# Splitting the left factors of the products of halves two at a time, from blocks side by side in one raw tile

## The chip, the cores and the metric

The kernel runs on one core of a Trainium2 chip. The time is device time in microseconds (us) of one execution; the kernel before took 1882.66 us, the median of 3 runs (1881.72 to 1883.4). One further execution was taken with the hardware profiler.

## What is computed

A decoder trunk of two layers on 512 tokens and 16 meta tokens in front of them, width 1024, everything in float32. Layer 0 mixes the tokens with gated linear attention, layer 1 with sliding-window attention on keys and values made after layer 0. Each layer has a feed-forward block (width 2816) before and after the mixer. Cut to what matters here:

```
def swiglu(x, w_in, w_out):
    gate, up = jnp.split(x @ w_in, 2, axis=-1)
    return (jax.nn.silu(gate) * up) @ w_out

for layer in range(DEPTH):
    h = h + 0.5 * rmsnorm(swiglu(rmsnorm(h, g[0]), w_ffn_in[layer, 0], w_ffn_out[layer, 0]), g[1])
    hn = rmsnorm(h, g[2])
    ...
    h = h + rmsnorm(mix, g[3])
    h = h + 0.5 * rmsnorm(swiglu(rmsnorm(h, g[4]), w_ffn_in[layer, 1], w_ffn_out[layer, 1]), g[5])
```

## The kernel before

**Operands in two parts.** TensorE multiplies in a reduced float32 format, so every operand is kept as a high part (the rounded value) and a low part (what is left), and each product is three matmuls: high by high, low by high, high by low. A weight comes from memory into a raw buffer by a DMA on SP's queue. ScalarE writes its high part (a copy with a rounding), and VectorE then writes its low part (raw less high). The text calls the two instructions a split. The pool `rp` has 8 raw buffers of 128 x 512, the pool `hp` 32 buffers of two times 528 columns ("slots", tag `pair`), which also hold the activations.

**The feed-forward block.** `ffn` works through the 22 hidden tiles of 128 in four chunks of 4, 6, 6 and 6 (`FF_CHUNKS`). After each chunk its part of the down projection follows (`out_steps`). The first chunk is computed plainly. The three others are the stretches that the change touches: there each hidden tile has a gate and an up weight (128 x 1024 each), and the two projections of the two halves of the tokens are computed with seven products of halves instead of eight (Strassen's scheme in the form with few additions). The left factors of the seven are sums of four blocks of the weights: r11 and r12 are the two halves of the gate weight, r21 and r22 those of the up weight. They have the names 11, 12, 22 and s1 = r21+r22, s3 = r11+r21, s2 = s3+r22, s4 = r12+s2. A product is 12 matmuls (4 blocks of 128 rows, three matmuls each), 264 columns wide in layer 0 and 256 in layer 1. The text calls a gate weight with its up weight a pair; a chunk has six pairs.

**The chain of a pair.** `split_pair` (L249) makes the seven factors: split 11, add r21 to r11 and r22 to r21 in place (L264), split s1, split s3, add r22 to r11, split s2, split 12, add r11 to r12, split s4, split 22. The high parts are L258, the low parts L259. In the profile the products' left factors that were added up are named `w_s`, the others `w`. For the other weights the split is L239 and L240.

**The products.** `Strassen.product` (L881) waits until a factor has been written out by the planner, issues the 12 matmuls and gives one slot back (`free_slots`). The order on TensorE is 11, s1, s2, 12, s3, then 11 of the next pair, then s4 and 22, so `head` (11), `body` and `tail` of two pairs interlock. Their results are gathered by L904 (a to d), L910, L912 and L914 on ScalarE and by L917, L926, L932 and L933 on VectorE; L927 is the SiLU, L936 and L937 write the hidden tile's two parts. L912 must have read bank a before s3 is added to it, L917 before 22 is.

**What sets the order.** TensorE's instructions run in the order of the program text. `Flow` is a planner at build time: its clock advances with every matmul, and jobs (generators) emit their instructions when their time has come; `yield STEP` puts 1.1 us of that clock between two steps of a chain. The other engines' instructions are put in order by the compiler, by readiness, starting from the order in which they were emitted; each engine then runs its list strictly in order. `load_unit` (L287) takes the next weight's raw buffers, issues its DMAs and starts its chain; `prefetch` calls it while the slots asked for stay within `ahead` (16) of those given back, with at most two chains of pairs at once (`CHAINS`). `slot` (L227) lets a chain take a slot only while fewer than the limit (`RING`, 10 in these stretches) are out. A raw buffer is given to the next load when its last reader is done.

Of the kernel before, what the change touches and what calls it, by code (L numbers as in the profile page):

```python
# [9 lines left out]
F32 = mybir.dt.float32  # L10
F32R = mybir.dt.float32r
I32 = mybir.dt.int32
AF = mybir.ActivationFunctionType
ALU = mybir.AluOpType
AX = mybir.AxisListType

P = 128
# [12 lines left out]
L1 = [(16, 256), (272, 256)]  # L30
L1W = [(16, 512)]
SLOTS = 32
RAWS = 8
RING = 10
STEP = 1.1
CHAINS = 2
# [101 lines left out]
def trunk_kernel(ctx: ExitStack, tc, a, out, last_out):  # L138
    nc = tc.nc
    pe, act, dve, pool, sp = nc.tensor, nc.scalar, nc.vector, nc.gpsimd, nc.sync  # L140
    flow = Flow()

    cp = ctx.enter_context(tc.tile_pool(name="cp", bufs=1))
    rp = ctx.enter_context(tc.tile_pool(name="rp", bufs=RAWS))
    hp = ctx.enter_context(tc.tile_pool(name="hp", bufs=SLOTS))
# [14 lines left out]
    def pair_tile(name, dt=F32R):  # L160
        return hp.tile([P, 2, TOK], dt, tag="pair", name=name)
# [5 lines left out]
    def flat(t):  # L167
        return t.rearrange("p a t -> p (a t)")
# [58 lines left out]
    def slot(i):  # L227

        while live[0] + sum(n for j, n in owed.items() if j < i) >= limit[0]:
            yield room[0]  # L230
        live[0] += 1
        owed[i] -= 1

    def raw_tile(name):
        return rp.tile([P, 512], F32, tag="raw", name=name)

    def split_part(i, raw, m):
        w = pair_tile(f"w{i}_{len(loaded[i])}")
# [7 lines left out]
            yield from slot(i)  # L246
            split_part(i, raw, m)

    def split_pair(i, raws):  # L249


        r11, r12, r21, r22 = raws
        parts, ready = loaded[i]

        def part(name, src):
            yield from slot(i)
            w = pair_tile(f"w{i}_{name}")
            act.activation(w[:, 0, :512], src, AF.Copy)  # L258
            dve.tensor_tensor(w[:, 1, :512], src, w[:, 0, :512].bitcast(F32), op=ALU.subtract)  # L259
            parts[name].append(w)  # L260
            ready[name].finish(flow)

        def add(dst, src):
            dve.tensor_tensor(dst, dst, src, op=ALU.add)  # L264

        yield 2.2
        yield from part("11", r11)
        add(r11, r21)
        add(r21, r22)
        yield STEP  # L270
        yield from part("s1", r21)
        yield STEP
        yield from part("s3", r11)
        add(r11, r22)
        yield STEP
        yield from part("s2", r11)
        yield STEP
        yield from part("12", r12)
        add(r12, r11)
        yield STEP  # L280
        yield from part("s4", r12)
        yield STEP
        yield from part("22", r22)
        chains[0] -= 1
        prefetch()

    def load_unit():  # L287
        i = len(loaded)
        asked[0] += costs[i]
        owed[i] = costs[i]  # L290
        if isinstance(units[i], list):
            g, u = units[i]
            chains[0] += 1
            raws = [raw_tile(f"raw{i}_{k}") for k in range(4)]
            for k in (2, 0, 1, 3):
                sp.dma_start(raws[k], (g, u)[k // 2][:, k % 2 * 512 : (k % 2 + 1) * 512])
                dma_end[0] = max(dma_end[0], flow.clock) + 512 * 1.5e-3
            names = ("11", "12", "22", "s1", "s2", "s3", "s4")
            loaded.append(({k: [] for k in names}, {k: Job(None) for k in names}))
            gen = split_pair(i, raws)  # L300
        else:
            n = units[i].shape[-1]
            raws = []
            for c in range(0, n, 512):
                m = min(512, n - c)
                raws.append((raw_tile(f"raw{i}_{c}"), m))
                sp.dma_start(raws[-1][0][:, :m], units[i][:, c : c + m])
            dma_end[0] = max(dma_end[0], flow.clock) + n * 1.5e-3
            loaded.append([])
            gen = split_unit(i, raws)  # L310
        split_jobs.append(flow.spawn(gen, dma_end[0] - flow.clock))

    def prefetch():
        while len(loaded) < cap[0] and asked[0] + costs[len(loaded)] <= freed[0] + ahead[0]:
            if isinstance(units[len(loaded)], list) and chains[0] == CHAINS:
                break
            load_unit()
# [16 lines left out]
    def free_slots(n):  # L334
        freed[0] += n
        live[0] -= n
        room[0].finish(flow)
        room[0] = Job(None)
        prefetch()
# [531 lines left out]
    class Strassen:  # L871
# [9 lines left out]
        def product(self, bank, t, left, right, first):  # L881
            parts, ready = t.pair
            flow.wait(ready[left])
            w = parts[left][0]
            for k in range(4):
                wh, wl = (w[:, i, k * P : (k + 1) * P] for i in range(2))
                xh, xl = (self.z[right][k // 2][:, i, k % 2] for i in range(2))
                mm(bank, wh, xh, first and k == 0, False, not first)
                mm(bank, wl, xh, False, False, not first)
                mm(bank, wh, xl, False, k == 3, not first)  # L890
                flow.pump()
            free_slots(1)

        def head(self, hid):
            t = Job(None)
# [571 lines left out]
    raws = [[raw_tile(f"raw{i}_{c}") for c in (0, 512)] for i in range(2)]  # L1467
# [156 lines left out]
```

## Time and profile before

| | us |
|---|---|
| median of 3 runs | 1882.66 |
| profiled execution | 1881.52 |
| its span, first to last instruction | 1879.7 |
| ScalarE: high parts of the pairs' factors (L258) | 175.2 + 133.9 |
| VectorE: low parts of the pairs' factors (L259) | 193.8 + 148.3 |
| VectorE: adds of blocks (L264) | 198.0 |
| VectorE waiting for the high parts of added factors | 128.7 |

The sums of L258 and L259 are over 288 factors `w_s` and 216 factors `w`, 72 pairs of seven. In the lines of the profile PE is TensorE's matmuls, PEld its weight loads, DVE VectorE, ACT ScalarE, POOL GpSimd and SP the engine that issues the DMAs. A line of a group has line, engine, operation, what is written and read, shapes and count, then busy time and mean duration of one in nanoseconds, then the idle time in front of them and whom the engine waited for. A line of a timeline has the start in us from the beginning of the span, the time taken, and the instruction; in brackets stands the idle time in front of it. Neighbouring instructions of one kind are merged, with their count. A matmul's duration there overlaps with its neighbours', so the distance of starts is what counts.

### The profile page before, as it was taken

The page shows a single profiled execution, that of the slowest core. Times are in us where ns is not written, and L with a number is a line of the kernel's source. Part 1 is how long each engine was busy: PE and PEld are TensorE (multiplying, and loading weights), DVE is VectorE, ACT ScalarE, POOL GpSimd, SP SyncE. Part 2 cuts the span into 40 slices and gives each one's busy share as a digit, 9 for nine tenths or more (in the row PEclk, how much of TensorE's full clock was granted, in tenths as well). Part 3 has the DMA queues.
Part 4 walks back from the last instruction along what each step waited for, and adds up shares of the span by engine and source line. Part 5 has one row for each costly group of instructions (what it writes and reads, how often), then busy time and mean ns, then how long its engine had stood idle before and what let it go on. Part 6 is the DMA issues. An engine that isn't in the chain of part 4 may idle for free.

```text
span 1879.7 us, 37270 instructions
## 1 busy us (share of the span) xinstructions
PE 1866.2 (99%) x14479; PEld 1784.8 (95%) x14479; DVE 1396.2 (74%) x2829; ACT 1026.9 (55%) x2311; POOL 163.9 (9%) x297
## 2 busy tenths in 40 slices
PE   9999999999999999999999999999999999999998
PEld 8999999999999999999999898989987898989898
DVE  7885858767564788585887886868766779868585
ACT  6663535654446566363574553536757855636364
POOL 2000000330001300000033000000320140000002
PEclk9999999999999999999999999999999999999999
DMA  5333233421213123232351223333421212333331
GB/s 170 99 96 101 92 105 96 138 68 57 68 57 113 46 90 108 90 102 91 109 168 46 73 88 110 93 110 101 136 74 52 69 46 73 99 104 104 102 113 60
DMA packets 102273, 174.70 MB, mean 93 GB/s; under 512 B 11856, under 2 KB 24016, under 8 KB 102096
## 3 DMA queue, kind: packets, MB, share of 16 engines
q1 hardware_dynamic: 101664, 171.74, 29.3%
q8 instruction: 113, 1.85, 0.4%
q10 hardware_dynamic: 432, 0.59, 0.1%
q14 instruction: 64, 0.52, 0.1%
HBM read 169.66 MB, written 2.10 MB: 91 GB/s over the span
## 4 chain that ended last, share of the span: by engine, by line
PE 85%; DVE 8%; ACT 4%; issue 2%; DMA 0%; POOL 0%; DVEq 0%; SPq 0%; ACTq 0%; POOLq 0%
PE y L175 31%; PE x L175 20%; PE a L175 17%; PE c L175 7%; PE d L175 4%; DVE raw L264 2%; ACT w_s L258 2%; DVE w_s L259 2%; DVE w L259 2%; PE o L175 1%; PE e L175 1%; PE po L175 1%; DVE w L240 1%; DVE hidl1f L937 1%; ACT s L1350 0%
## 5 line engine op out<-in xcount | busy, mean ns | idle before, releaser
L259 DVE TENSOR_TENSOR w_s<-raw,w_s 128x512 fp32r<-128x512 f32 x288 | 193.8, 690 | 131.0 <-ACT w_s L258 128.7
L175 PE MATMUL y<-hidl0f,w 128*128 128x256 f32 (+1 forms) x2112 | 261.4, 285 | 0.3 <-DVE hidl0f L451 0.3
L175 PEld LDWEIGHTS y<-hidl0f,w 128*128 128x128 f32 x2112 | 259.0, 188 | 0.7 <-DVE hidl0f L451 0.5
L240 DVE TENSOR_TENSOR w<-raw,w 128x512 fp32r<-128x512 f32 x376 | 235.3, 654 | 31.3 <-ACT w L239 29.1
L258 ACT ACTIVATE w_s<-raw 128x512 fp32r<-128x512 f32 x288 | 175.2, 628 | 152.3 <-DVE raw L264 139.5
L175 PE MATMUL y<-hidl1f,w 128*128 128x512 f32 (+1 forms) x1344 | 251.2, 346 | 0.4 <-DVE hidl1f L937 0.3
L175 PEld LDWEIGHTS y<-hidl1f,w 128*128 128x128 f32 x1344 | 212.5, 188 | 35.1 <-DVE hidl1f L937 1.6
L239 ACT ACTIVATE w<-raw 128x512 fp32r<-128x512 f32 x376 | 207.0, 586 | 41.4 <-PE y L175 29.3
L264 DVE TENSOR_TENSOR raw<-raw,raw 128x512 f32<-128x512 f32 x288 | 198.0, 687 | 5.5
L445 POOL TENSOR_TENSOR acc_post<-acc_post,sq_post 128x256 f32<-128x256 f32 (+1 forms) x77 | 63.3, 822 | 1537.1 <-ACT sq_post L444 1536.4
L259 DVE TENSOR_TENSOR w<-raw,w 128x512 fp32r<-128x512 f32 x216 | 148.3, 687 | 30.0 <-ACT w L258 29.2
L258 ACT ACTIVATE w<-raw 128x512 fp32r<-128x512 f32 x216 | 133.9, 621 | 41.6 <-PE y L175 41.3
L175 PE MATMUL x<-x_l0m,w 128*128 128x272 f32 (+1 forms) x1152 | 152.0, 288 | 0.0
L175 PEld LDWEIGHTS x<-x_l0m,w 128*128 128x128 f32 x1152 | 143.2, 188 | 2.7 <-issue 1.7
L701 DVE TENSOR_TENSOR Y<-y,Y 128x256 f32<-128x256 f32 (+2 forms) x175 | 81.8, 474 | 71.2 <-PE y L175 70.8
L175 PE MATMUL a<-zl0f_t,w_s 128*128 128x264 f32 x864 | 117.3, 285 | 0.0
L175 PE MATMUL a<-zl1f_t,w_s 128*128 128x256 f32 x864 | 114.3, 281 | 1.1 <-ACT c L912 0.7
L175 PEld LDWEIGHTS a<-zl0f_t,w_s 128*128 128x128 f32 x864 | 110.1, 188 | 0.3
L175 PEld LDWEIGHTS a<-zl1f_t,w_s 128*128 128x128 f32 x864 | 107.2, 188 | 2.9 <-ACT c L912 2.6
L175 PE MATMUL x<-x_l0f,w 128*128 128x256 f32 (+1 forms) x768 | 98.1, 287 | 1.2 <-ACT w L239 0.7
L175 PEld LDWEIGHTS x<-x_l0f,w 128*128 128x128 f32 x768 | 94.8, 188 | 2.5 <-DVE w L240 1.1
L175 PE MATMUL x<-x_l1f,w 128*128 128x256 f32 (+1 forms) x576 | 93.1, 320 | 0.0
(516 smaller groups left out, 3219.9 us busy)
## 6 DMA issues: line engine op xcount, KB each, us to landing
raw<-in_w_in SPq DMA_DIRECT2D x352, 256.0 KB, 2.9
raw<-in_w_out SPq DMA_DIRECT2D x96, 256.0 KB, 3.3
raw<-in_w_last SPq DMA_DIRECT2D x48, 256.0 KB, 3.0
raw<-in_gla_in SPq DMA_DIRECT2D x48, 256.0 KB, 3.3
raw<-in_w_out SPq DMA_DIRECT2D x64, 128.0 KB, 2.9
raw<-in_gla_out SPq DMA_DIRECT2D x16, 256.0 KB, 2.7
raw<-in_w_q SPq DMA_DIRECT2D x16, 256.0 KB, 4.2
raw<-in_swa_out SPq DMA_DIRECT2D x16, 256.0 KB, 3.4
```

Of the source, the lines that this page charges most:

```text
L175: inst = pe.matmul(o, lhs, rhs, start=start, stop=stop, skip_group_check=onto)
L239: act.activation(w[:, 0, :m], raw[:, :m], AF.Copy)
L240: dve.tensor_tensor(w[:, 1, :m], raw[:, :m], w[:, 0, :m].bitcast(F32), op=ALU.subtract)
L258: act.activation(w[:, 0, :512], src, AF.Copy)
L259: dve.tensor_tensor(w[:, 1, :512], src, w[:, 0, :512].bitcast(F32), op=ALU.subtract)
L264: dve.tensor_tensor(dst, dst, src, op=ALU.add)
L445: pool.tensor_tensor(sums[0][:, :n], sums[0][:, :n], t[:, :n], op=ALU.add)
L701: dve.tensor_tensor(y, p[:, :n], y, op=ALU.add)
L937: dve.scalar_tensor_tensor(t.hid[:, 1, g], t.h, -1.0, t.hid[:, 0, g].bitcast(F32), op0=ALU.mult, op1=ALU.subtract)
```

## The change

The raw pool has two tiles of 2048 columns in place of eight of 512. `raw_tile` hands out quarters of the current tile; a pair takes a whole one. A pair's four blocks lie in it in the order r21, r11, r12, r22, in which they are also loaded. `split_pair` splits 11 alone, as before, and then two factors at a time, from two blocks that lie side by side: s1 with s3, s2 with 12, s4 with 22. Each is one ScalarE instruction and one VectorE instruction of 1024 columns. The high parts of two factors go into one slot and their low parts into another. The adds stay as they were. `product` takes the high and low part from two places, and gives slots back when both factors that share them are used: one after 11, two after 12, s3 and 22. In the planner's time the steps of the chain lie where the first factor of each two lay.

```diff
--- before.py
+++ after.py
@@ -30,7 +30,7 @@
 L1 = [(16, 256), (272, 256)]
 L1W = [(16, 512)]
 SLOTS = 32
-RAWS = 8
+RAWS = 2
 RING = 10
 STEP = 1.1
 CHAINS = 2
@@ -231,8 +231,15 @@
         live[0] += 1
         owed[i] -= 1
 
-    def raw_tile(name):
-        return rp.tile([P, 512], F32, tag="raw", name=name)
+    quarters = [None, 4]
+
+    def raw_tile(name, n=1):
+
+        if quarters[1] + n > 4:
+            quarters[:] = rp.tile([P, 2048], F32, tag="raw", name=name), 0
+        t, i = quarters
+        quarters[1] += n
+        return t[:, i * 512 : (i + n) * 512]
 
     def split_part(i, raw, m):
         w = pair_tile(f"w{i}_{len(loaded[i])}")
@@ -246,41 +253,42 @@
             yield from slot(i)
             split_part(i, raw, m)
 
-    def split_pair(i, raws):
-
-
-        r11, r12, r21, r22 = raws
+    def split_pair(i, raw):
+
+
+
         parts, ready = loaded[i]
-
-        def part(name, src):
-            yield from slot(i)
-            w = pair_tile(f"w{i}_{name}")
-            act.activation(w[:, 0, :512], src, AF.Copy)
-            dve.tensor_tensor(w[:, 1, :512], src, w[:, 0, :512].bitcast(F32), op=ALU.subtract)
-            parts[name].append(w)
-            ready[name].finish(flow)
+        r21, r11, r12, r22 = (raw[:, k * 512 : (k + 1) * 512] for k in range(4))
+
+        def two(names, k):
+            hi, lo = [], []
+            n = len(names)
+            for _ in names:
+                yield from slot(i)
+            ws = [flat(pair_tile(f"w{i}_{name}")) for name in names]
+            hi, lo = (ws[0][:, :1024], ws[1][:, :1024]) if n == 2 else (ws[0][:, :512], ws[0][:, 512:1024])
+            src = raw[:, k * 512 : (k + n) * 512]
+            act.activation(hi, src, AF.Copy)
+            dve.tensor_tensor(lo, src, hi.bitcast(F32), op=ALU.subtract)
+            for c, name in enumerate(names):
+                parts[name] += [t[:, c * 512 : (c + 1) * 512] for t in (hi, lo)]
+                ready[name].finish(flow)
 
         def add(dst, src):
             dve.tensor_tensor(dst, dst, src, op=ALU.add)
 
         yield 2.2
-        yield from part("11", r11)
+        yield from two(["11"], 1)
         add(r11, r21)
         add(r21, r22)
         yield STEP
-        yield from part("s1", r21)
-        yield STEP
-        yield from part("s3", r11)
+        yield from two(["s1", "s3"], 0)
         add(r11, r22)
-        yield STEP
-        yield from part("s2", r11)
-        yield STEP
-        yield from part("12", r12)
+        yield 2 * STEP
+        yield from two(["s2", "12"], 1)
         add(r12, r11)
-        yield STEP
-        yield from part("s4", r12)
-        yield STEP
-        yield from part("22", r22)
+        yield 2 * STEP
+        yield from two(["s4", "22"], 2)
         chains[0] -= 1
         prefetch()
 
@@ -291,13 +299,13 @@
         if isinstance(units[i], list):
             g, u = units[i]
             chains[0] += 1
-            raws = [raw_tile(f"raw{i}_{k}") for k in range(4)]
-            for k in (2, 0, 1, 3):
-                sp.dma_start(raws[k], (g, u)[k // 2][:, k % 2 * 512 : (k % 2 + 1) * 512])
+            raw = raw_tile(f"raw{i}", 4)
+            for c, k in enumerate((2, 0, 1, 3)):
+                sp.dma_start(raw[:, c * 512 : (c + 1) * 512], (g, u)[k // 2][:, k % 2 * 512 : (k % 2 + 1) * 512])
                 dma_end[0] = max(dma_end[0], flow.clock) + 512 * 1.5e-3
             names = ("11", "12", "22", "s1", "s2", "s3", "s4")
             loaded.append(({k: [] for k in names}, {k: Job(None) for k in names}))
-            gen = split_pair(i, raws)
+            gen = split_pair(i, raw)
         else:
             n = units[i].shape[-1]
             raws = []
@@ -881,15 +889,14 @@
         def product(self, bank, t, left, right, first):
             parts, ready = t.pair
             flow.wait(ready[left])
-            w = parts[left][0]
             for k in range(4):
-                wh, wl = (w[:, i, k * P : (k + 1) * P] for i in range(2))
+                wh, wl = (w[:, k * P : (k + 1) * P] for w in parts[left])
                 xh, xl = (self.z[right][k // 2][:, i, k % 2] for i in range(2))
                 mm(bank, wh, xh, first and k == 0, False, not first)
                 mm(bank, wl, xh, False, False, not first)
                 mm(bank, wh, xl, False, k == 3, not first)
                 flow.pump()
-            free_slots(1)
+            free_slots({"11": 1, "12": 2, "s3": 2, "22": 2}.get(left, 0))
 
         def head(self, hid):
             t = Job(None)
```

## The prediction

> **What bounds the kernel now.** I read the page's busy times first, then the waits of the weight loads, then busy time by stretch, and then the timelines of VectorE, ScalarE and TensorE inside two stretches of products of halves.
>
> ```profile
> PE 1866.2 (99%) x14479; PEld 1784.8 (95%) x14479; DVE 1396.2 (74%) x2829; ACT 1026.9 (55%) x2311; POOL 163.9 (9%) x297
> PEld a L175 <- ACT c L912: 2.6, 7, 0.9
> 179.70:236.90 57.20, 57.20 (x472) 57.20 (x471) 45.27 (x81) 32.90 (x69) 0.00 (x0) 1.00 0.29 88
> 1169.20:1225.50 56.30, 56.25 (x474) 55.93 (x473) 45.56 (x82) 32.93 (x71) 0.00 (x0) 1.00 0.29 88
> ```
>
> TensorE (PE) bounds the time: it is busy 99% of the span. The two windows are a stretch of six pairs in layer 0 and one in layer 1 (columns: window and length, then busy time of PE, weight load, VectorE, ScalarE, GpSimd, then granted clock). There are twelve such stretches, three in each of four feed-forward blocks, and they are the only places where the changed code works. PE never stops in the first and hardly in the second, at full clock. The one wait that the list has for the weight loads of these products is for L912, 2.6 us together. So a change of the splits can win next to nothing; the question is whether it can lose, that is, by how much the splits are ahead of PE, and what paces them.
>
> ```profile
> 197.21 1.64 PE L175 MATMUL a<-zl0f,w 128*128 128x264 f32 x12
> 203.09 1.64 PE L175 MATMUL a<-zl0f_t,w_s 128*128 128x264 f32 x12
> 207.51 1.62 PE L175 MATMUL a<-zl0f,w 128*128 128x264 f32 x12
> 213.35 1.62 PE L175 MATMUL a<-zl0f_t,w_s 128*128 128x264 f32 x12
> 227.99 1.63 PE L175 MATMUL a<-zl0f,w 128*128 128x264 f32 x12
> 199.90 0.69 DVE L259 TENSOR_TENSOR w_s<-raw,w_s 128x512 fp32r<-128x512 f32 x1 [0.77 <-ACT w_s L258]
> 205.40 1.42 DVE L264 TENSOR_TENSOR raw<-raw,raw 128x512 f32<-128x512 f32 x2
> 207.52 1.29 DVE L259 TENSOR_TENSOR w_s<-raw,w_s 128x512 fp32r<-128x512 f32 x2 [0.70 <-ACT w_s L258]
> 208.73 0.42 DVE L917 TENSOR_TENSOR c<-a,c 128x264 f32<-128x264 f32 x1
> 209.07 0.68 DVE L264 TENSOR_TENSOR raw<-raw,raw 128x512 f32<-128x512 f32 x1
> 210.45 0.69 DVE L259 TENSOR_TENSOR w_s<-raw,w_s 128x512 fp32r<-128x512 f32 x1 [0.70 <-ACT w_s L258]
> ...
> 214.60 0.70 DVE L937 SCALAR_TENSOR_TENSOR hidl0f<-c,hidl0f 128x528 fp32r<-128x528 f32 x1
> 215.24 0.69 DVE L259 TENSOR_TENSOR w<-raw,w 128x512 fp32r<-128x512 f32 x1
> 215.96 1.42 DVE L264 TENSOR_TENSOR raw<-raw,raw 128x512 f32<-128x512 f32 x2
> 206.86 1.16 ACT L258 ACTIVATE w_s<-raw 128x512 fp32r<-128x512 f32 x2 [0.23 <-DVE raw L264]
> ```
>
> These are timelines of layer 0: start, duration, instruction, and in brackets how long the engine had stood idle and for whom. PE starts factor 11 of a pair at 197.21, 207.51 and, two pairs later, at 227.99: (227.99-197.21)/3 = 10.26 us for a pair. VectorE starts its two opening adds at 205.40 and again at 215.96: **10.56 us** for a pair. VectorE is the slower of the two although it is idle a fifth of the time: it stands in a chain. An add ends, ScalarE writes the high part, only then can VectorE subtract for the low part, then comes the next add. So the lead that the splits have at the start of a stretch is used up. Factor s2 is done at 199.90+0.69 = 200.59 and used at 203.09 in the third pair: 2.50 us ahead; in the fourth it is done at 211.14 and used at 213.35: 2.21 ahead.
>
> ```profile
> 1092.32 1.58 PE L175 MATMUL a<-zl1f,w 128*128 128x256 f32 x12
> 1112.18 1.59 PE L175 MATMUL a<-zl1f,w 128*128 128x256 f32 x12
> 1128.07 1.58 PE L175 MATMUL a<-zl1f_t,w_s 128*128 128x256 f32 x12
> 1110.99 1.42 DVE L264 TENSOR_TENSOR raw<-raw,raw 128x512 f32<-128x512 f32 x2
> 1112.38 0.42 DVE L917 TENSOR_TENSOR c<-a,c 128x256 f32<-128x256 f32 x1
> 1113.11 1.29 DVE L259 TENSOR_TENSOR w_s<-raw,w_s 128x512 fp32r<-128x512 f32 x2 [0.30 <-ACT w_s L258]
> 1121.31 1.42 DVE L264 TENSOR_TENSOR raw<-raw,raw 128x512 f32<-128x512 f32 x2
> 1126.63 0.70 DVE L259 TENSOR_TENSOR w_s<-raw,w_s 128x512 fp32r<-128x512 f32 x1 [0.37 <-ACT w_s L258]
> ```
>
> In layer 1 a product is narrower, and PE takes (1112.18-1092.32)/2 = 9.93 us for a pair; the sixth pair's s2 is done at 1127.33 and used at 1128.07, **0.74 us ahead**. The compiler's order also shows here: as VectorE falls behind PE, L917 moves into the wait in front of the subtraction (0.70 becomes 0.30), and the step from add to add is 1121.31-1110.99 = 10.32 us.
>
> **The change part by part.** Of the seven high parts and seven low parts of a pair, six of each become three of double width: three instructions fewer on each engine, and the adds stay.
>
> ```profile
> L1016 ACT ACTIVATE az<-az x2: 1088/1088/1089, 415.5 to 418.1; 128x1056 f32<-128x1056 f32 x2
> L1240 DVE TENSOR_TENSOR dv<-vt x1: 941/941/941, 1034.5 to 1034.5; 128x768 f32<-128x768 f32 x1
> L258 ACT ACTIVATE w_s<-raw 128x512 fp32r<-128x512 f32 x288 | 175.2, 628 | 152.3 <-DVE raw L264 139.5 <-PE y L175 12.5
> L259 DVE TENSOR_TENSOR w_s<-raw,w_s 128x512 fp32r<-128x512 f32 x288 | 193.8, 690 | 131.0 <-ACT w_s L258 128.7 <-PE d L175 0.7
> ```
>
> No row has these instructions at 1024 columns, so I work them out. ScalarE: 628 ns at 512 columns and 1088 at 1056 is 0.85 ns a column, so 1.06 us; it can't be under 628 ns nor much over the 1.16 us of two in a row (206.86). VectorE: 690 ns at 512 and 941 at 768 is 0.98 ns a column, so 1.20 us, between 0.94 and the 1.29 us of two in a row.
>
> *The step of one chain.* Before, from the end of an add (205.40+1.42 = 206.82) to the end of both subtractions (207.52+1.29 = 208.81) it was 1.99 us, and the first factor was there after 1.39 (208.21). After, ScalarE starts 0.04 later, works 1.06, VectorE follows 0.03 behind it and works 1.20: 2.33 us, with both factors only then. So each double step costs **0.34 us more in the chain**, though it saves 0.09 us of VectorE's work, and the factor used first comes 0.94 us later. Three double steps make a pair's chain 1.02 us longer: 10.56+1.02 = 11.58 in the same order. In the order in which evacuations fill the waits it is less. A wait now has room (1.06+0.07 = 1.13 us) for the 0.34 us steps of L917 and L926 (208.73 to 209.07), so two of the three waits can each take one: 11.58-0.68 = 10.90. From the period that is filled already, 10.32+1.02 = 11.34. I take **11.2 us**, nearer to the second, whose order was measured.
>
> *What PE then waits.*
>
> ```profile
> 192.72 0.71 DVE L937 SCALAR_TENSOR_TENSOR hidl0f<-c,hidl0f 128x528 fp32r<-128x528 f32 x1 [0.71 <-ACT hidl0f L936]
> ```
>
> For s2 of the third pair of a layer 0 stretch the lead of 2.50 loses 0.94 (half a step), 0.34 (the s1 and s3 step in front) and 0.3 that the second pair leaves behind (its three steps are 1.02 longer, and L937 at its end stood idle for 0.71 anyway; bounds 0 and 1.0): 0.92 is left. Each later pair loses 11.2-10.26 = 0.94, so the sixth is at 0.92-2.82 = -1.9: PE has waited 1.9 us by the end of the stretch.
>
> ```profile
> 1094.98 0.69 DVE L259 TENSOR_TENSOR w_s<-raw,w_s 128x512 fp32r<-128x512 f32 x1 [0.70 <-ACT w_s L258]
> 1098.02 1.58 PE L175 MATMUL a<-zl1f_t,w_s 128*128 128x256 f32 x12
> ```
>
> In layer 1 the same lead is 1098.02-1095.67 = 2.35, 0.77 after the same losses, and 11.2-9.93 = 1.27 go in each later pair: -3.0. Six stretches of each: 6 x 1.9 + 6 x 3.0 = **29 us**.
>
> *Slots.* Two factors share two slots, and these come free together, after 12, s3 and 22, where each product freed its own. By the next load's condition (a pair is asked for when s3 has freed its share) the count is the same then as before, so loads are asked for at the same products. A lump needs both slots: s2 with 12 needs those freed after 12, and its place in the order, 2.2 of the planner's us after s1 with s3, lies behind that. I cost this at nothing; if it binds, one product (10.26/7 = 1.47 us) is late once a stretch, 18 us at most.
>
> *The raw tile.* One tile for a pair comes free only at its last split, where each quarter had its own buffer.
>
> ```profile
> DMA to landing us min/median/max: 2.2/3.0/6.5
> 208.24 6.80 SPq L296 DMA_DIRECT2D raw<-in_w_in  x4
> 218.80 6.80 SPq L307 DMA_DIRECT2D raw<-in_w_out  x4
> 236.77 2.04 PE L175 MATMUL y<-hidl0f,w 128*128 128x272 f32 x15
> ```
>
> So the four loads for the pair after next start where 22 is split (before L937, about 214.7) and not from 208.24 on. At the slowest landing of any raw load they are there at about 223 (four issues in some 2 us, then 6.5). Factor 11 of that pair is split at 215.24+10.56 = 225.8. The cover is 3 us, and a longer chain adds to it; cost nothing. On SP's queue the down-projection loads stand behind: from 218.80 they move to about 226, land by 232 and are used from 236.77; split in under 2 us, they are in time by 2 to 3 us, and PE's own lag adds to that. For the other weights a load can now wait for up to three more quarters; their splits run several units ahead under the slot limit, cost nothing. Products, matmuls and operands of PE stay as they are: 0.
>
> *The rule that bears on it.* The Trainium skill, Perfetto Trace Analysis, Optimizing Scalar/DVE Operations, says that grouping into larger operations helps throughput where the engine is saturated, and that where it isn't but makes others wait, smaller instructions let work finish sooner. VectorE is busy 45.27 of 57.20 us here, 79%, so this case falls under the second half, which speaks against the change; by the first half it would be the second rival's case.
>
> *Behind the waiting instructions.* On VectorE L917, L926, L932 and L933 stand behind a waiting subtraction, on ScalarE L904, L910 and L912 behind a longer activation or one that waits for an add; PE waits for L917 before product 22 and for L912 before s3. They are late by the same chain, so PE pays once, and I add nothing.
>
> **Sum.** The profiled execution took 1881.52 us (span 1879.7), 1.1 under the median of 1882.66. 1881.52+29 = 1910.5; I forecast **1911 us**, on the median's side.
>
> **Rivals.**
> 1. *The order stays as in the row at 207.52*, nothing fills the longer waits, and the second pair leaves 0.8 behind: 11.58 a pair. Layer 0: 2.50-0.94-0.34-0.8 = 0.42, less 3 x 1.32 = -3.5; layer 1: 0.27, less 3 x 1.65 = -4.7; 49 us, 1932. For it: the layer 0 period shown is unfilled. Against: order follows readiness, and with longer waits more is ready.
> 2. *Not slower: the grouping frees VectorE.* Its work for a pair falls by 0.27 us, and if the compiler places the next pair's 11 and opening adds (0.69 and 1.42 us) in the longer waits, the three waits of 1.13 us are filled and the chain of two pairs overlaps. It decides from a step of at most 9.9 us a pair. VectorE is busy 45.3/6 = 7.5 us a pair, so there is room. Then PE sees nothing, and at best the 2.6 us for L912 go: 1880 to 1884. Against: with these factors already loaded, no period shown moved them up.
> 3. *Late transfers* through the one raw tile: it decides from landings over 9 us, which no row shows; then, at one us a stretch, 1895.
>
> **How the numbers follow.** Forecast 0.55 (10.8 to 11.5 us a pair by the working above: 15 to 40 us, 1897 to 1923), first rival 0.20 (1923 to 1942, more if the double widths cost their upper bounds), second 0.22, third 0.03. About 0.2% (3.8 us) is what a measurement of this kernel can tell from no change. The second rival splits into 0.17 within that and 0.05 faster; all others are slower, 0.78. The range 1882 to 1942 leaves out the lower half of the second rival and the far end of the first, 0.16 together.
>
> **What would show it.** Right: double-width rows of about 1.06 us on ScalarE and 1.20 on VectorE; opening adds 10.9 to 11.6 us apart; PE waits for the low parts in the fourth to sixth pairs, more in layer 1; VectorE's busy time some 20 us lower in all; stages between unchanged. Wrong: opening adds as close as PE's pairs, or the next pair's 11 subtracted between an add and its double step, so that no product waits; or ScalarE far under 1 us at 1024 columns.

## The result and the profile after

The changed kernel takes **1938.82 us** (median of 4 runs, 1938.3 to 1940.36), the kernel before beside it 1882.19 (4 runs, 1881.54 to 1883.4): ratio 1.0302, interval 1.029 to 1.0314. It is slower by 57 us; the forecast was slower by 29. The profiled span is 1937.2 us.

The page of the changed kernel, busy times and the groups of the change (in its kernel.py the splits of pairs are L271 and L272, the adds L278; L904, L910, L912, L914, L917, L926, L927, L932, L933, L936 and L937 are now L911, L917, L919, L921, L924, L933, L934, L939, L940, L943 and L944; L239 and L240, the split of the other weights, are L246 and L247):

```profile
PE 1889.0 (98%) x14479; PEld 1791.4 (92%) x14479; DVE 1380.6 (71%) x2613; ACT 1001.4 (52%) x2095; POOL 161.7 (8%) x297
L271 ACT ACTIVATE w_s<-raw 128x1024 fp32r<-128x1024 f32 x216 | 229.0, 1060 | 291.7 <-DVE raw L278 277.0
L272 DVE TENSOR_TENSOR w<-raw,w_s 128x1024 fp32r<-128x1024 f32 x144 | 176.3, 1224 | 82.8 <-ACT w_s L271 71.6
L272 DVE TENSOR_TENSOR w_s<-raw,w_s 128x1024 fp32r<-128x1024 f32 x72 | 88.2, 1225 | 87.1 <-ACT w_s L271 82.9
```

Both engines have less work than before (VectorE 15.6 us less, ScalarE 25.5) and yet the program is slower. The wide instructions take 1.06 and 1.22 us. What has grown is ScalarE's wait for the adds, 277.0 us, where L258 `w_s` had 139.5.

The list of waits of the weight loads, for products and down projections (whom, us in total, times, longest):

```profile
PEld a L175 <- ACT c L919: 20.2, 30, 0.9
PEld a L175 <- DVE w L272: 15.2, 30, 0.7
PEld y L175 <- DVE hidl0f L944: 5.3, 10, 0.8
```

TensorE now waits in two places of a pair: in s2 for its low part, and before s3 for L919, the copy that must have read bank a. The last row is a down projection that waits for a hidden tile. The same two stretches as in the prediction, up to the first matmul of the down projection, before the change and after it:

```profile
179.70:236.77 57.07, 57.07 (x471) 57.07 (x469) 45.14 (x81) 32.77 (x69) 0.00 (x0) 1.00 0.29 88
1169.20:1224.78 55.58, 55.53 (x470) 55.33 (x469) 44.84 (x80) 32.21 (x69) 0.00 (x0) 1.00 0.28 86
```

```profile
183.15:242.59 59.44, 58.12 (x470) 57.26 (x469) 43.04 (x64) 30.24 (x53) 0.00 (x0) 1.00 0.22 67
1199.42:1258.59 59.17, 56.77 (x470) 55.55 (x469) 43.29 (x64) 29.89 (x53) 0.00 (x0) 1.00 0.25 81
```

The layer 0 stretch is 2.37 us longer, the layer 1 stretch 3.59, at full clock. Taken from the starts of all of TensorE's matmuls in the two traces, first product to last, the twelve stretches are 44.5 us longer in sum (on average 3.45 in layer 0, 3.96 in layer 1); the down projections behind them are 10.7 us longer, nearly all of it behind the last stretch of a block (1.8, 2.8, 3.6 and 1.5); some 2 us lie elsewhere.

One pair of layer 0 on VectorE, the timeline of the changed kernel:

```profile
109.59 1.42 DVE L278 TENSOR_TENSOR raw<-raw 128x512 f32<-128x512 f32 x2
110.93 0.43 DVE L924 TENSOR_TENSOR c<-a,c 128x264 f32<-128x264 f32 x1
112.14 1.23 DVE L272 TENSOR_TENSOR w_s<-raw,w_s 128x1024 fp32r<-128x1024 f32 x1 [0.79 <-ACT w_s L271]
113.40 0.69 DVE L278 TENSOR_TENSOR raw<-raw 128x512 f32<-128x512 f32 x1
114.01 0.43 DVE L933 TENSOR_TENSOR c<-c,c 128x264 f32<-128x264 f32 x1
115.22 1.23 DVE L272 TENSOR_TENSOR w<-raw,w_s 128x1024 fp32r<-128x1024 f32 x1 [0.78 <-ACT w_s L271]
116.36 0.43 DVE L939 TENSOR_TENSOR c<-a,c 128x264 f32<-128x264 f32 x1
116.71 0.68 DVE L278 TENSOR_TENSOR raw<-raw 128x512 f32<-128x512 f32 x1
117.31 0.43 DVE L940 TENSOR_TENSOR c<-c 128x264 f32<-128x264 f32 x1
118.52 1.22 DVE L272 TENSOR_TENSOR w<-raw,w_s 128x1024 fp32r<-128x1024 f32 x1 [0.78 <-ACT w_s L271]
...
121.00 1.42 DVE L278 TENSOR_TENSOR raw<-raw 128x512 f32<-128x512 f32 x2
```

Three times VectorE finishes an add, waits out a whole wide activation (end of the adds at 111.01, next subtraction at 112.14) with one short evacuation in the gap, subtracts for 1.23 us, and adds again. From opening add to opening add it is 121.00-109.59 = **11.41 us**. Apart from L924, L933 and L940, which run inside the waits, VectorE does one thing after the other in that time; the three dots stand for L944 and the low part of the next 11.

The timeline of TensorE and then of ScalarE at the same place:

```profile
110.59 1.62 PE L175 MATMUL a<-zl0f,w 128*128 128x264 f32 x12
120.14 1.74 PE L175 MATMUL a<-zl0f_t,w_s 128*128 128x264 f32 x12 [0.55 <-ACT c L919]
121.72 1.51 PE L175 MATMUL a<-zl0f,w 128*128 128x264 f32 x11
```

```profile
117.42 1.06 ACT L271 ACTIVATE w_s<-raw 128x1024 fp32r<-128x1024 f32 x1 [1.92 <-DVE raw L278]
118.39 0.63 ACT L943 ACTIVATE hidl0f<-c 128x528 fp32r<-128x528 f32 x1
118.92 0.37 ACT L917 ACTIVATE c<-c 128x264 f32<-128x264 f32 x1
119.19 0.62 ACT L271 ACTIVATE w<-raw 128x512 fp32r<-128x512 f32 x1
119.72 0.38 ACT L919 ACTIVATE c<-a 128x264 f32<-128x264 f32 x1
```

This is the fourth pair. From its 11 to the next pair's 11 TensorE takes 121.72-110.59 = 11.13 us where it took 10.24. It stands before s3 until L919 has run. L919 is fourth in ScalarE's list behind the wide activation of s4 and 22, which itself has waited 1.92 us for an add.

### The profile page after: what moved, and what is told of

Same layout as the page of the kernel before. It is cut to its first block, busy times and chain, and to the rows that moved or that the text cites. A ratio compares the mean times of both kernels' runs of the same rounds, so it can differ in the third digit from the quotient of the medians.

```text
span 1937.2 us, 36550 instructions
## 1 busy us (share of the span) xinstructions
PE 1889.0 (98%) x14479; PEld 1791.4 (92%) x14479; DVE 1380.6 (71%) x2613; ACT 1001.4 (52%) x2095; POOL 161.7 (8%) x297
## 4 chain that ended last, share of the span: by engine, by line
PE 62%; DVE 20%; ACT 11%; issue 4%; DMA 3%; SPq 0%; POOL 0%; DVEq 0%; ACTq 0%; POOLq 0%
PE y L175 26%; PE x L175 19%; ACT w_s L271 7%; PE a L175 7%; DVE w L272 6%; DVE raw L278 6%; PE c L175 3%; DVE w_s L272 3%; PE d L175 1%; DVE w L247 1%; DMA raw<-in_w_last 1%; PE o L175 1%; PE po L175 1%; DMA raw<-in_w_in 1%; DMA raw<-in_w_out 1%
## 5 line engine op out<-in xcount | busy, mean ns | idle before, releaser
L271 ACT ACTIVATE w_s<-raw 128x1024 fp32r<-128x1024 f32 x216 | 229.0, 1060 | 291.7 <-DVE raw L278 277.0
L247 DVE TENSOR_TENSOR w<-raw,w 128x512 fp32r<-128x512 f32 x376 | 234.6, 653 | 64.3 <-ACT w L246 62.2
L246 ACT ACTIVATE w<-raw 128x512 fp32r<-128x512 f32 x376 | 205.9, 585 | 73.7 <-DMA raw<-in_w_out 29.3
L272 DVE TENSOR_TENSOR w<-raw,w_s 128x1024 fp32r<-128x1024 f32 x144 | 176.3, 1224 | 82.8 <-ACT w_s L271 71.6
L278 DVE TENSOR_TENSOR raw<-raw 128x512 f32<-128x512 f32 x288 | 198.4, 689 | 6.3
L175 PE MATMUL a<-zl0f_t,w_s 128*128 128x264 f32 x1008 | 178.0, 286 | 8.5 <-ACT c L919 6.9
L175 PE MATMUL a<-zl1f_t,w_s 128*128 128x256 f32 x1008 | 173.3, 282 | 7.8 <-ACT c L919 7.0
L175 PEld LDWEIGHTS a<-zl1f_t,w_s 128*128 128x128 f32 x1008 | 146.9, 188 | 12.0 <-ACT c L919 10.8
L272 DVE TENSOR_TENSOR w_s<-raw,w_s 128x1024 fp32r<-128x1024 f32 x72 | 88.2, 1225 | 87.1 <-ACT w_s L271 82.9
L175 PE MATMUL a<-zl1f_t,w 128*128 128x256 f32 x288 | 82.8, 287 | 8.1 <-DVE w L272 8.1
```

Of the source, the lines that this page charges most:

```text
L175: inst = pe.matmul(o, lhs, rhs, start=start, stop=stop, skip_group_check=onto)
L246: act.activation(w[:, 0, :m], raw[:, :m], AF.Copy)
L247: dve.tensor_tensor(w[:, 1, :m], raw[:, :m], w[:, 0, :m].bitcast(F32), op=ALU.subtract)
L271: act.activation(hi, src, AF.Copy)
L272: dve.tensor_tensor(lo, src, hi.bitcast(F32), op=ALU.subtract)
```

## The experiments

Times are medians; the kernel before stood at 1882.2 to 1883.0 us beside them. Runs 1 to 8 start from the changed kernel or take over its raw tile. Line numbers shift by a few from kernel to kernel: L924, L925, L926 and L929 of the runs below are L917 of the kernel before, the evacuation that must have read bank a before product 22. Three dots in an edit stand for lines left out.

**1. Narrow instructions in the changed kernel's frame.** Raw tile, slots in twos and planner steps stay; each factor has its own two instructions.

```diff
-            act.activation(hi, src, AF.Copy)
-            dve.tensor_tensor(lo, src, hi.bitcast(F32), op=ALU.subtract)
+            for c in range(n):
+                q = slice(c * 512, (c + 1) * 512)
+                act.activation(hi[:, q], src[:, q], AF.Copy)
+                dve.tensor_tensor(lo[:, q], src[:, q], hi[:, q].bitcast(F32), op=ALU.subtract)
```

> The changed kernel with its raw tile, slots and planner times, but every factor split with its own 512-wide activation and subtraction. Theory A (a double-width activation and subtraction run one behind the other, so the chain add, high parts, low parts, add grows to 11.4 us a pair, over TensorE's 10.2 and 9.9): the opening adds are 10.3 to 10.6 us apart again, the twelve stretches lose at most 5 us against before instead of 44, and only what is lost behind the last stretch of each block (10.7 us in the changed kernel) may stay: 1883 to 1895 us. Theory B (the whole-tile release of the raw tile, or slots that come free in twos, makes the factors late): the loss stays, 1925 us or more.

Measured **1880.78 us** (10 runs, ratio 0.9991, 0.9981 to 1.0). The whole loss goes, that of the down projections too, although the raw tile and the slots in twos are still there. So it comes from the width of the splits; what it is about the width, the next runs must tell.

**2 and 3. One of the two wide.** In the second run only ScalarE's instruction keeps 1024 columns, in the third only VectorE's; the edits are one half of that of run 1 each.

```diff
             act.activation(hi, src, AF.Copy)
-            dve.tensor_tensor(lo, src, hi.bitcast(F32), op=ALU.subtract)
+            for c in range(n):
+                q = slice(c * 512, (c + 1) * 512)
+                dve.tensor_tensor(lo[:, q], src[:, q], hi[:, q].bitcast(F32), op=ALU.subtract)
```

```diff
-            act.activation(hi, src, AF.Copy)
+            for c in range(n):
+                q = slice(c * 512, (c + 1) * 512)
+                act.activation(hi[:, q], src[:, q], AF.Copy)
             dve.tensor_tensor(lo, src, hi.bitcast(F32), op=ALU.subtract)
```

> The changed kernel with 1024-wide activations but two 512-wide subtractions behind each. Theory A: the step from an add to both low parts is 0.04+1.06+0.03+1.29 = 2.42 us, as long as in the changed kernel (2.36), so opening adds 11.3 to 11.6 us apart and 1930 to 1945 us, a little less where the first low part, now 0.6 us earlier, was what TensorE waited for. Theory C (it is the long activation that holds L919's copy in ScalarE's queue, and TensorE waits for that): the same, 1930 to 1945. Theory D (it is the long subtraction): 1883 to 1895.

> The changed kernel with two 512-wide activations and one 1024-wide subtraction behind them. Theory A: the step is 0.04+1.16+0.03+1.23 = 2.46 us, opening adds 11.4 to 11.7 us apart, 1935 to 1950 us. Theory C (the long activation in ScalarE's queue): no long activation is left, so the waits for L919 go, 1885 to 1910. Theory D (the long subtraction): 1930 to 1945.

Measured **1952.17** (wide activation, one run) and **1903.24** (wide subtraction, one run). The wide activation alone is worse than both together: two short subtractions behind it make a step 0.07 us longer than one long. The wide subtraction alone costs over a third of the loss; its largest wait is of another kind, that of run 4:

```profile
PEld a L175 <- DVE c L926: 11.2, 7, 2.3
```

The expectation that the chain's length alone decides (1935 to 1950 for run 3) fell: two short activations in a row take 1.16 us, more than a long one with its 1.06, and yet this version loses less. Its trace shows an earlier start: ScalarE starts the first of the two at 109.48, while VectorE is still at the second of the opening adds (108.75 to 110.17), and from opening adds to opening adds it is 10.41 us there, not 11.41. Run 6 takes this up.

**4. The raw tile alone.** The kernel before with two raw tiles of 2048 columns, a pair's blocks side by side in one, its splits, slots and steps untouched.

```diff
-RAWS = 8
+RAWS = 2
...
-            raws = [raw_tile(f"raw{i}_{k}") for k in range(4)]
+            raw = raw_tile(f"raw{i}", 4)
+            raws = [raw[:, c * 512 : (c + 1) * 512] for c in (1, 2, 0, 3)]
```

> The kernel before with the raw tile of the change alone: two tiles of 2048 columns, a pair's four blocks side by side in one of them; splits, slots and adds as before. Theory A: the stretches stay within 3 us of before in sum. If the 10.7 us lost behind the last stretch of each block come from loads that wait for a whole tile, they show here too, 1886 to 1893 us; if they come from the lag of the wide splits, 1881 to 1885. Theory B (the raw tile makes the factors late): the stretches lose 20 us or more, 1902 us or more.

Measured **1909.41 us** (4 runs, ratio 1.0144, 1.0127 to 1.016). So the tile is not free by itself. The timelines say where it costs: SP's queue from 132 us on, VectorE and TensorE, at the end of the first stretch, first in the kernel before, then in this one:

```profile
132.69 11.43 SPq L307 DMA_DIRECT2D raw<-in_w_out  x12
144.14 0.42 DVE L917 TENSOR_TENSOR c<-a,c 128x264 f32<-128x264 f32 x1
144.88 1.61 PE L175 MATMUL a<-zl0f_t,w 128*128 128x264 f32 x12
```

```profile
139.57 9.80 SPq L315 DMA_DIRECT2D raw<-in_w_out  x12
143.95 1.03 DVE L247 TENSOR_TENSOR w<-raw,w 128x512 fp32r<-128x512 f32 x2 [2.30 <-ACT w L246]
146.22 0.69 DVE L247 TENSOR_TENSOR w<-raw,w 128x512 fp32r<-128x512 f32 x1 [1.24 <-ACT w L246]
146.83 0.42 DVE L925 TENSOR_TENSOR c<-a,c 128x264 f32<-128x264 f32 x1
147.31 1.74 PE L175 MATMUL a<-zl0f_t,w 128*128 128x264 f32 x12 [2.08 <-DVE c L925]
```

Before, a transfer for the down projection went out whenever one of the eight buffers came free. Now SP's queue issues none between 132 and 139.57, until a whole tile is free, and then a run of them. Here it isn't the down projection that misses them: VectorE has their subtractions in its list ahead of L925, stands there 2.30 and 1.24 us, and L925 must have read bank a before product 22 is added to it. TensorE stops for 2.08 us. Such stops make the twelve stretches 13.1 us longer in sum. Nearly all the rest, some 13 us, lies in the down projections, most of it behind the last stretch of a block: there TensorE waits for the last hidden tile (L944 and L945), and behind the third stretch one sees its evacuations queued behind splits of late weights in the same way.

**5. Tiles of two blocks.** As run 4, but r21 with r11 in one raw tile and r12 with r22 in another (four tiles of 1024 columns).

```diff
-RAWS = 2
+RAWS = 4
...
-        if quarters[1] + n > 4:
-            quarters[:] = rp.tile([P, 2048], F32, tag="raw", name=name), 0
+        if quarters[1] + n > 2:
+            quarters[:] = rp.tile([P, 1024], F32, tag="raw", name=name), 0
...
-            raw = raw_tile(f"raw{i}", 4)
-            raws = [raw[:, c * 512 : (c + 1) * 512] for c in (1, 2, 0, 3)]
+            two = [raw_tile(f"raw{i}_{h}", 2) for h in range(2)]
+            raws = [two[c // 2][:, c % 2 * 512 : (c % 2 + 1) * 512] for c in (1, 2, 0, 3)]
```

> The kernel before with raw tiles of two blocks (r21 with r11, r12 with r22) in place of one tile of four. Theory D (the whole raw tile costs because the down projection's transfers can't start before the pair's last split): half of them start two splits earlier, 1884 to 1900. Rival (the tile costs by something else): 1906 to 1912, as with four blocks in a tile.

Measured **1887.8 us** (7 runs, ratio 1.0025, 1.0014 to 1.0036). The queue goes on earlier, and most of the stop is gone:

```profile
135.92 8.50 SPq L315 DMA_DIRECT2D raw<-in_w_out  x12
145.40 1.73 PE L175 MATMUL a<-zl0f_t,w 128*128 128x264 f32 x12 [0.39 <-DVE c L925]
```

So it is the time of release. In run 1, with the whole tile, the queue stands too, but only until 136.44, and no product waits in this stretch (in the others 2.9 us in all, for L926): there the splits are done early enough.

**6. Narrow, but ScalarE in the order of the text.** As run 1, but s3's high part is held behind s1's, 12's behind s2's and 22's behind s4's (`after(a, b)` tells the compiler to put b behind a).

```diff
-                act.activation(hi[:, q], src[:, q], AF.Copy)
+                inst = act.activation(hi[:, q], src[:, q], AF.Copy)
+                if c:
+                    after(prev, inst)
+                prev = inst
```

> The narrow splits in the changed kernel's frame, but ScalarE is held to the order of the text within each two: s1's high part ahead of s3's, s2's ahead of 12's, s4's ahead of 22's. Theory A (early start of the factor that is ready): VectorE waits for high parts again (over 120 us), and the time goes to 1895 to 1912, with narrow instructions. Rival B (only the length of the instructions counts): 1878 to 1884, as without the order.

Measured **1903.31 us** (2 runs, ratio 1.0109, 1.009 to 1.0127). VectorE's waits for high parts, first the second row of the kernel before (its first is in the prediction, 128.7 us), then run 1, then this run:

```profile
DVE w L259 <- ACT w L258: 29.2, 30, 1.9
```

```profile
DVE w_s L274 <- ACT w_s L273: 27.8, 9, 3.7
DVE w L274 <- ACT w L273: 22.3, 38, 1.9
DVE w L274 <- ACT w_s L273: 4.8, 7, 2.1
```

```profile
DVE w_s L277 <- ACT w_s L273: 62.3, 63, 3.6
DVE w L277 <- ACT w_s L273: 48.8, 77, 1.5
DVE w L277 <- ACT w L273: 14.9, 18, 1.8
```

Before the change it was 158 us, in run 1 it is 55, and here 126 again, with the same narrow instructions. So run 1 was fast because one factor of each two doesn't need the add that its neighbour waits for, and was started first. A wide instruction can't do that: it waits for the later of its two operands. The order of the text isn't dear by itself, though: the kernel before has it too, and so has run 11 below, with a raw buffer for every block, at 1889.59 us. It is dear together with the raw tile: TensorE's largest wait here is the one of run 4, for L929, 6.5 us, and run 4 has this order and this tile as well (1909.41).

**7. The adds first.** Wide splits, but with no add between one and the next: 11 with 22 first, then three adds in a row, then s1 with s3 and s2 with 12 on end. The blocks lie as r21, r11, r22, r12.

```diff
-        yield from two(["11"], 1)
+        yield from two(["11", "22"], 1)
         add(r11, r21)
         add(r21, r22)
+        add(r22, r11)
...
-        add(r11, r22)
...
-        yield from two(["s2", "12"], 1)
-        add(r12, r11)
+        yield from two(["s2", "12"], 2)
+        add(r12, r22)
...
-        yield from two(["s4", "22"], 2)
+        yield from two(["s4"], 3)
...
-                set_ahead(16, RING)
+                set_ahead(18, RING)
...
-            free_slots({"11": 1, "12": 2, "s3": 2, "22": 2}.get(left, 0))
+            free_slots({"12": 2, "s3": 2, "s4": 1, "22": 2}.get(left, 0))
```

As 11 now shares its slots with 22, these are given back later, and loads may run ahead by two slots more (18 for 16). That this limit alone does nothing wasn't tried.

> Wide splits kept, but no longer one add between each two: blocks lie as r21, r11, r22, r12; 11 with 22 is split first, then the three adds for s3, s1 and s2 follow each other, then s1 with s3, s2 with 12 (its operand is ready by then), the last add, and s4 alone. Theory A (a wide split costs because it stands between two adds that wait for each other): PE's waits in the stretches go, 1878 to 1892. Rival B (long instructions hold up what is queued behind them on ScalarE and VectorE, whatever the chain): 1915 or more.

Measured **1885.86 us** (8 runs, ratio 1.0018, 1.0008 to 1.0028), with instructions as long as in the changed kernel. VectorE there:

```profile
109.90 2.15 DVE L278 TENSOR_TENSOR raw<-raw 128x512 f32<-128x512 f32 x3
...
112.45 1.23 DVE L272 TENSOR_TENSOR w_s<-raw,w_s 128x1024 fp32r<-128x1024 f32 x1
113.59 1.22 DVE L272 TENSOR_TENSOR w<-raw,w_s 128x1024 fp32r<-128x1024 f32 x1
...
120.12 2.14 DVE L278 TENSOR_TENSOR raw<-raw 128x512 f32<-128x512 f32 x3
```

The second wide subtraction follows the first without a wait, and the pair takes 120.12-109.90 = 10.22 us, TensorE's own pace. Eleven of the twelve stretches keep the length of before within 0.6 us; one is 3.1 longer, at its end, where TensorE waits for L924 as in run 4.

**8. L919 on VectorE.** The changed kernel with that copy moved off ScalarE's list.

```diff
-            act.activation(t.u2, t.a, AF.Copy)
+            dve.tensor_copy(t.u2, t.a)
```

> The changed kernel, with the copy of s2 out of its bank (L919, for which PE waits 34 us before s3) on VectorE in place of ScalarE. Theory C (its place in ScalarE's list behind long activations is a wait of its own): that wait goes and little takes its place, 1904 to 1925. Prediction's step (late by the same chain, PE pays once): the same time is then waited for the low parts, and VectorE has 0.43 us more a pair to do: 1937 to 1965.

Measured **1952.65 us** (2 runs). The wait stays with the copy, and is longer (the pair takes 122.16-110.54 = 11.62 us from opening add to opening add):

```profile
PEld a L175 <- DVE c L919: 55.2, 48, 1.9
```

So it isn't the copy's place in ScalarE's list alone: on VectorE it stands between the low part of 11 and the opening adds, in the chain itself, and either list moves at the chain's pace. This run alone couldn't refute that long activations are a cause of their own; run 7 does, where the copy stays on ScalarE, the activations are as long, and the wait for L919 is 0.9 us in all.

**9 to 11. What lets the compiler start the ready factor first.** All three have the raw buffers of before, eight of 512 columns, and narrow splits. Run 9 is the kernel before with the steps of a chain grouped as in the change:

```diff
-        yield STEP
         yield from part("s3", r11)
...
-        yield STEP
+        yield 2 * STEP
         yield from part("s2", r11)
-        yield STEP
         yield from part("12", r12)
...
```

> The kernel before, with its own buffer for every block and its narrow splits; only the steps of a chain are emitted in the grouping of the change (s1 with s3, s2 with 12, s4 with 22, two planner steps between groups). Theory A (what made the narrow splits in the changed kernel's frame as fast as before is that the compiler may start, of each two, the factor whose operand is ready, and the grouped emission lets it): VectorE's wait for high parts falls from 158 us to under 80, and the time is 1877 to 1882. Rival (the side-by-side blocks or the pairwise slots did it): the wait stays near 158 us and the time at 1880 to 1884.

Measured **1896.29 us** (5 runs, ratio 1.0069, 1.0055 to 1.0083): the theory missed; the rival had the wait right and the time too low.

Run 10 is run 1 with these buffers (high parts of two factors share a tile, and so do their low parts).

```diff
-RAWS = 2
+RAWS = 8
...
-            raw = raw_tile(f"raw{i}", 4)
+            raw = [raw_tile(f"raw{i}_{k}") for k in range(4)]
```

> The narrow splits of the changed kernel's frame (pairwise slots; high parts of two factors in one tile, low parts in another), but with a raw buffer for every block, as before the change. Theory: the pairwise tiles, taken for both factors before the first is split, are what lets the compiler start s3, 12 and 22 early; the raw tile isn't. Then VectorE waits under 80 us for high parts, no stretch is longer, and the time is 1876 to 1882. Rival: the side-by-side raw tile lets them start early; then the wait is 120 us or more again and the time 1880 to 1896.

Measured **1878.63 us** (11 runs, ratio 0.9978, 0.9969 to 0.9987), **below both kernels**.

Run 11 is run 10 with a factor's high and low part in one tile again, as before:

```diff
-                act.activation(hi[:, q], raw[k + c], AF.Copy)
+                act.activation(w[:, :512], raw[k + c], AF.Copy)
...
-                dve.tensor_tensor(lo[:, q], raw[k + c], hi[:, q].bitcast(F32), op=ALU.subtract)
+                dve.tensor_tensor(w[:, 512:1024], raw[k + c], w[:, :512].bitcast(F32), op=ALU.subtract)
```

> As the version with a raw buffer for every block and pairwise slots, but high and low part of a factor in the factor's own tile again, as before the change; both tiles are still taken ahead of both splits. It separates what the early start of s3, 12 and 22 needs. If taking both tiles ahead is enough: VectorE waits under 80 us for high parts and the time is 1877 to 1881. If it is the sharing of a tile by two high parts (the compiled lists of the two engines point this way: s1 ahead of s3, s2 ahead of 12, s4 ahead of 22): the wait is 120 us or more, the sixth pairs lose about 1 us as with the grouped steps alone, and the time is 1884 to 1898.

Measured **1889.59 us** (5 runs, ratio 1.004, 1.0026 to 1.0055). VectorE's largest wait for high parts in runs 9, 10 and 11:

```profile
DVE w_s L259 <- ACT w_s L258: 131.1, 173, 3.6
```

```profile
DVE w_s L266 <- ACT w_s L265: 27.5, 8, 3.6
```

```profile
DVE w_s L263 <- ACT w_s L262: 131.1, 169, 3.6
```

Only run 10 loses it. ScalarE's compiled list shows the order by the buffers' names, run 10 first, as most pairs have it (raw_0 is r21, raw_1 r11, raw_2 r12, raw_3 r22), then run 11:

```
w_s<-raw_1   w_s<-raw_0   w_s<-raw_2   w_s<-raw_1   w_s<-raw_3   w_s<-raw_2
w_s<-raw_0   w_s<-raw_1   w_s<-raw_1   w_12<-raw_2  w_s<-raw_2   w_22<-raw_3
```

The first is s3, s1, 12, s2, 22, s4, the second s1, s3, s2, 12, s4, 22. On VectorE in run 10 the pair has no wait for a high part after the one for factor 11:

```profile
118.85 1.42 DVE L272 TENSOR_TENSOR raw<-raw,raw 128x512 f32<-128x512 f32 x2
120.24 1.50 DVE L266 TENSOR_TENSOR w_s<-raw,w_s 128x512 fp32r<-128x512 f32 x2
...
122.60 1.28 DVE L266 TENSOR_TENSOR w<-raw,w_s 128x512 fp32r<-128x512 f32 x2
...
129.07 1.42 DVE L272 TENSOR_TENSOR raw<-raw,raw 128x512 f32<-128x512 f32 x2
```

So what decides the order is which parts share a tile; taking both tiles ahead isn't enough (run 11), nor are the steps (run 9), and the raw tile isn't needed (run 10). Whether it counts that the two high parts share one, or that a factor's high and low part don't, isn't told apart, and why the compiler picks the ready factor only then stays open. In runs 9 and 11 about 1 us is lost in the sixth pair of eight stretches, and run 9 has one wait of 3.6 us more; their cause is open too.

## Why the prediction was right, and where it was too small

**Right:** the sign and the mechanism. The measured time lies in the stated range, 1882 to 1942, but only through the band that was left for the first rival (1923 to 1942); the forecast's own band ended at 1923, and what carried the time past it is told below. The durations were 1.06 us (forecast 1.06) and 1.22 (1.20). The Trainium skill, VectorE: DVE Perf Modes, section on the TRN2 errata, gives (N+151)/0.96 ns for a float32 addition of two tensors; for 1024 columns that makes an estimate of 1224 ns, and this trace has 1224 and 1225 for the subtraction. The step of the chain, from the adds' end at 111.01 to 112.14+1.23 = 113.37, is 2.36 us (forecast 2.33). TensorE waits in the fourth to sixth pairs, as said, and VectorE's busy time fell by 15.6 us (forecast some 20).

**A pair's period: 11.41, not 11.2.** The forecast let the evacuations fill the longer waits. Three do (L924, L933, L940), but L939 runs at 116.36 between a wide subtraction and the add behind it, and so lengthens the chain by 0.35 us. With each of the three steps 0.03 us longer than forecast, too, the period lies 0.21 us above the 11.2 that was taken between 10.90 and 11.34; in layer 1 it is as long (11.38).

**"They are late by the same chain, so PE pays once, and I add nothing."** That it is one chain is shown by run 7: with the chain broken both waits went. In run 8 the wait for L919 went along with it to the other engine. But the lead was counted at the low part of s2 alone. L919's lead is the smaller one and is used up first, so the fourth pair already takes 0.89 us longer. Up to the down projection the two stretches shown lost 2.37 and 3.59 us where 1.9 and 3.0 were forecast. With the last products of a stretch it is 44.5 us in all, against 29.

**"The raw tile ... cost nothing."** This step failed. The forecast looked at TensorE's use of the down projection's weights and not at what stands behind their subtractions in VectorE's list; alone the tile costs 27 us (run 4), and the time of its release is the cause (run 5). Late transfers were the third rival, but by landings over 9 us; in the changed kernel the raw tile's landings take 3.9 us in the median and 6.6 at most, so the cost comes without slow ones. Of the changed kernel's loss 10.7 us lie in the down projections, and the late transfers can be seen there: at the end of the third stretch ScalarE stands 1.48, 0.63 and 1.47 us for weights (splits at 346.04, 348.05 and 350.16), and L934, which the last hidden tile needs and whose operand was there at 349.74, runs behind them at 351.38. Late last splits come on top, and the two weren't separated; run 1, which has the tile and an early chain, loses nothing in the down projections. The slots in twos, put at nothing as well, do cost nothing in run 1.

**The rivals.** The first, an unfilled order at 11.58 us a pair, gave 1932: nearest in the total, but with a longer period than the measured one and nothing for the tile. The second, that the next pair's 11 and opening adds fill the waits, did not come: in the pair shown they run behind the last wide subtraction. Starting early what is ready does help the narrow instructions (run 1, 55 us of waits in place of 158); a wide one waits for the later operand.

The Trainium skill, Perfetto Trace Analysis, Optimizing Scalar/DVE Operations, has it that breaking up instructions may let work finish sooner where an engine isn't saturated but holds up another. The trace agrees: VectorE is 71% busy, and the same frame takes 1880.78 us in short instructions and 1938.82 in long. Runs 6 and 7 add that length isn't the point: short ones in the order of the text cost 21 us with the raw tile (7 with a buffer for every block, run 11), and long ones without an add between them 3.

| what | us against before |
|---|---|
| narrow, ready factor first, own buffers (run 10) | -4.2 |
| narrow, ready factor first, one raw tile (run 1) | -1.4 |
| wide, adds first (run 7) | +3.3 |
| narrow, order of the text, own buffers (run 11) | +6.6 |
| narrow, order of the text, one raw tile (run 6) | +20.7 |
| kernel before with one raw tile (run 4) | +27 |
| wide, an add between each two (the change) | +56.6 |

## What to carry to other kernels

Before two instructions are made one, ask which of their operands is ready first: the wide one starts with the later, and in a chain that goes back and forth between two engines this costs more than the fixed time saved, though both engines have less to do. Put the steps that depend on each other on end on one engine (here the adds), and the width is nearly free. A buffer that several blocks share comes free with the last of them; look for the loss not at the reader of the late data, but at what stands behind that data's first use in an engine's list.

## What had not been expected of the hardware and the order

ScalarE's activation of 128 x 1024 took 1060 ns, where two of 512 columns in a row take 1.16 us, and VectorE's subtraction 1224 ns against 1.28: the width itself saves 0.1 us and less, much as forecast. Not expected was the order: in which order the compiler put the same instructions hung on which of them share a tile. Runs 10 and 11 differ in nothing else and lie 11 us apart, more than the width could have won, as TensorE waited 2.6 us in all for these products in the kernel before.
